# First up projection of a transformer block: one group of modulation columns computed on GpSimd, block products from feature tile 6 instead of 8

## The chip, the core and the metric

The kernel runs on one core of a Trainium2 chip. A core has TensorE (PE in the profile; PEld is its weight load), VectorE (DVE), ScalarE (ACT), GpSimd (POOL) and SyncE (SP, which issues the transfers). They run their own instruction streams, each in order, and wait for each other through semaphores. The metric is device time in microseconds: the median of 3 runs of the kernel before is 1021.51 us (1021.45 to 1022.29).

## The reference, cut to what matters

One layer of a streaming encoder on 512 frames of width 1024: a gated feed-forward net, a token mixer, a second gated feed-forward net. Before each, the input is normalised and scaled and shifted by columns that a linear layer makes from one conditioning vector `c`.

```python
sc = jax.nn.silu(c)
mod = sc @ w_ada[l] + b_ada[l]                # 1024 x (9 * 1024)
sh1, s1, g1, sh2, s2, g2, sh3, s3, g3 = jnp.split(mod, N_MOD, axis=-1)
h = _modulate(x, sh1, s1)                     # rms(x) * (1 + s1) + sh1
x = x + 0.5 * g1 * _swiglu(h, ffn1_w_in[l], ffn1_w_out[l])
# _swiglu: gate, up = split(h @ w_in, 2);  (silu(gate) * up) @ w_out
```

`sh1` and `s1` are needed before anything else. The other seven vectors (14 pieces of 512 columns) are needed later: `g1` when the first feed-forward net's output is added to `x`, the rest after that. A "group" is four pieces, so group 0 is `g1` and `sh2`.

## The kernel before, in words

Everything is kept transposed: features on the 128 partitions, the 512 frames along the row. The hidden width of the feed-forward net, 2816, is 22 feature tiles of 128. For each tile f the gate part and the up part need a product of a 1024 x 128 slice of weights with the 1024 x 512 input `h`. Products are in float32 accuracy made of three reduced products: weights and input are each split into a high and a low part, and high*high, high*low and low*high are added up in PSUM (`mm3`). ScalarE rounds to the high part, VectorE subtracts to get the low part.

The first up projection (`ffn1`) has four stages. `phase0` makes the shift and scale, the input and tiles 0 to 2. `plain` makes tiles directly: per tile 2 parts x 8 slices x 3 = 48 matmuls of 512 columns (L475 to L477). `by_sevens` makes tiles by a Strassen-like scheme: the gate and up weights and the two halves of the frames form a 2 x 2 block product, done with seven products instead of eight, each 4 slices x 3 = 12 matmuls of 256 columns, so 84 per tile (L360). The seven products need sums and differences of the inputs, made once (`combined`: tiles t, th, tl), and of the weights, made for each tile (`sevenths`, one tile ahead, in place in the weight buffers wr, and split into wh, wl, sh, sl). Last, tile 21 is plain again while the activations are split. Before, tiles 3 to 7 are plain and 8 to 20 go by sevens.

The modulation columns of group 0 are made as side work. `ada_rest` loads pieces of `w_ada` (128 x 512, tile ar), multiplies each by its entry of `sc` and accumulates eight of them into a sum aa, all on VectorE: L842 for the first, L844 for the others, 32 instructions for the group. `ada_columns` then lets TensorE add up the partitions of the four sums (L866), ScalarE copy the result and TensorE transpose it (L873), and VectorE add the bias. Before, the sums of group 0 stand between the matmuls of plain tiles 3 to 6 and the columns in tile 7.

What sets the order: side work is a Python generator, and `Rates` decides how many of its steps are placed between two pieces of main work. From the code written in that order a scheduler makes each engine's stream. Most 128 x 512 tiles share 56 slots (`slots`); a tile that gets a used slot waits for the slot's last reader. Weight tiles wr have four buffers, so the pair of tile f+2 is loaded when that of tile f is no longer read. All these transfers stand in one queue, SP's.

Of the kernel before, what the change touches and what calls it, by code (L numbers as in the profile page):

```python
# [11 lines left out]
F32 = mybir.dt.float32  # L12
# [4 lines left out]
ALU = mybir.AluOpType  # L17
AX = mybir.AxisListType

P = 128  # L20
NT = 512
D = 1024
KT = D // P
# [3 lines left out]
EPS = 1e-6  # L27
HALF = NT // 2
KPARTS = ((0, 8), (8, 8), (16, 6))
SEVEN = range(8, 21), range(4, 21)  # L30
PAD = 112
SEVENS = 0, 1
PLAN = (("all", 0), ("all", 1), ("tail", 4), ("tail", 5), ("tail", 6), ("tail", 7), (0, 4), (0, 6), ("most", 2), ("most", 3),
# [66 lines left out]
class Block:  # L100
# [712 lines left out]
        return self.rsqrt(ve, n)  # L813


    def ada_rest(self, groups, late=False):


        nc = self.nc
        a1 = self.ins["w_ada"][0]  # L820
        waiting = None

        def pair(kc, o):
            src = a1[kc * P:(kc + 2) * P, o:o + NT]
            if late:
                a = [self.slot(s="ar") for _ in range(2)]
                for e in range(2):
                    self.load(a[e], src[e * P:(e + 1) * P])
                return a
            a = self.early.tile([P, 2, NT], F32, tag="ar", name=self.name("ar"), bufs=3)  # L830
            self.load(a, src.rearrange("(k p) n -> p k n", p=P))
            return [a[:, e] for e in range(2)]

        for g in groups:
            accs = []
            for c in range(4 * g, min(4 * g + 4, 14)):
                acc = self.slot(s="aa")
                for kc in range(0, KT, 2):
                    for e, a in enumerate(pair(kc, 2 * D + c * NT)):
                        sc = self.sc[:, kc + e:kc + e + 1]  # L840
                        if kc + e == 0:
                            nc.vector.tensor_scalar(out=acc, in0=a, scalar1=sc, scalar2=None, op0=ALU.mult)  # L842
                        else:
                            nc.vector.scalar_tensor_tensor(out=acc, in0=a, scalar=sc, in1=acc, op0=ALU.mult, op1=ALU.add)  # L844
                    yield
                    if waiting and kc in (2, 4):
                        if next(waiting, "end") == "end":
                            waiting = None
                accs.append(acc)
            waiting = self.ada_columns(g, accs)  # L850
        if not late:
            self.columns = waiting
            return
        yield
        yield
        for _ in waiting:
            yield
            yield
# [59 lines left out]
    def ffn1(self):  # L918
        with self.tc.tile_pool(name="p0", bufs=3) as self.p0:
            with self.in_order():  # L920
                pu = self.phase0()
        self.late_pool = self.tc.tile_pool(name="early", bufs=4)
        self.early = self.late_pool.__enter__()
        with self.behind():
            act = [self.glu(pu[f], pu[3 + f], whole=True) for f in range(3)]
        side, sums = Side(), Side()
        side.add(self.ada_rest((0,)))
        sums.add(self.combined())
        with self.behind():
            self.plain(act, 3, 4, Rates((side,), (0.75,)))  # L930
            self.plain(act, 4, 6, Rates((side, sums), (0.75, 1)))
        self.plain(act, 6, 7, Rates((side, sums), (1, 1)))
        side.flush()
        self.late_exit()
        self.seven_enter()
        side.add(self.columns)
        self.plain(act, 7, 8, Rates((sums, side), (1, 0.1)), True)
        sums.flush()
        side.flush()
        self.by_sevens(act, SEVEN[0])  # L940
        return act

    def plain(self, act, f0, f1, side, last=False):
# [14 lines left out]
        self.late_pool = self.tc.tile_pool(name="seven", bufs=2)  # L958
        self.seven = self.late_pool.__enter__()

    def by_sevens(self, act, fs):

        side, self.last_queued = Side(), None

        def first():
            yield
            yield
            self.prefetch(1)

        for f in fs:  # L970
            w = self.weights7
            if f + 1 in fs:
                side.add(self.next_unit(ahead=0))
            else:
                side.add(first())
            if f + 2 == fs.stop:
                self.preload(2)
            with self.queued(mybir.EngineType.Activation, self.last_queued):
                act.append(self.seven_products(w, side))
                side.flush()  # L980
        self.late_exit()
        self.late_enter(12)
        last = fs[-1] + 1
        self.whole = act[:8]

        def parted():
            for i in range(last):
                act[i] = self.glu_parts(act[i], 8 <= i < 14)
                yield

        side.add(parted())
        for f in range(last, FT):
            p = []
            for _ in range(2):
                u, q = self.next_unit(), self.acc()
                for k in (0, 4):
                    self.dense(q, u, self.h, k0=k, k1=k + 4)
                    side.step(3)
                p.append(q)
            act.append(self.glu(*p))  # L1000
        self.splits = side

    def down(self, act, gate, norm=None):
# [27 lines left out]

        last = KT - 1
        side, held = Side(), []
        side.add(self.ada_rest((1, 2) if norm else (3,), True))
        if norm:
            self.consts = Side()
            self.consts.add(self.mixer_consts())
# [98 lines left out]
    def last_down(self, act, gate):  # L1136

        nc = self.nc
        full = slice(0, NT)
        side, sums, parts7, ended, held = Side(), Side(), Side(), [], []  # L1140
        side.add(self.ada_rest((3,), True))
        sums.add(self.act_sums(self.whole))

        def update(t, ts, src):
            nc.vector.scalar_tensor_tensor(out=self.xT[t][:, ts], in0=src, scalar=self.mod[gate][:, t:t + 1],
                                           in1=self.xT[t][:, ts], op0=ALU.mult, op1=ALU.add)

        def ahead():
            self.preload(1)
            parts7.add(self.raws.pop(0)())  # L1150

        def stores():
            while ended:
                self.store(ended.pop(0), range(NB))
                yield

        for at, (kind, t) in enumerate(PLAN):
            after = [k for k, _ in PLAN[at + 1:at + 3]] + ["all"] * 2
            if kind in SEVENS:
                w, work = self.weights7, parts7  # L1160
                if after[0] in SEVENS:
                    ahead()
                else:
                    work = Side()
                    work.add(self.readied())
                self.seven_down(w, act, 8 * kind, t, update, work, stores())
                work.flush()
                if kind:
                    ended += [t, t + 1]
                elif after[0] not in SEVENS:  # L1170
                    sums.add(self.act_sums(act[8:16]))
                continue
            p = self.acc()
            for i, (k0, n) in enumerate(KPARTS):
                if i in MISSING[kind]:
                    continue
                u = self.next_unit(ahead=0 if i == 2 and after[0] in SEVENS else 1)
                if kind == "tail" and after[0] == "tail" and after[1] in SEVENS or (
                        i == (0 if kind == "most" else 1) and after[0] in SEVENS):
                    ahead()  # L1180
                if at == 2:
                    side.flush()
                for k in range(0, n, 2):
                    while not at and any(not isinstance(a, tuple) for a in act[:k0 + k + 5]):
                        self.splits.step()
                    for j in range(k, k + 2):
                        xh, xl = act[k0 + j]
                        self.mm3(p, u[0][:, j, :], u[1][:, j, :], xh, xl, k0 + j == (16 if kind == "tail" else 0),
                                 k0 + j == FT - 1)
                    if at == 1:  # L1190
                        side.step()
                    if at > 1 or i == 2 and at:
                        sums.step()
                    parts7.step()
                if ended and kind != "tail":
                    self.store(ended.pop(0), range(NB))
            held.append((t, p))
            if at > 1:
                for h, p in held:
                    update(h, full, p)  # L1200
                    if kind == "all" or h < 2:
                        ended.append(h)
                held = []
            if after[0] in SEVENS:
                sums.flush()
                parts7.flush()
# [1296 lines left out]
```

## Time and profile before

| | |
|---|---|
| median of 3 runs | 1021.51 us |
| the profiled execution | 1021.74 us, span 1020.0 us |
| TensorE (PE) busy | 1010.3 us, 99% |
| VectorE (DVE) busy | 809.1 us, 79% |
| ScalarE (ACT) busy | 513.5 us, 50% |
| GpSimd (POOL) busy | 28.9 us, 3% |
| plain tiles of the first up projection | about 58 to 114 us |
| tiles by sevens | about 114 to 245 us |

Times in a view are microseconds from the start of the span, mean durations of one instruction are in nanoseconds. Matmuls overlap, so the time of a row of them is read from start to start, not from the duration of one. A row of the windows view gives for a stretch its length and, for each engine, busy time and the number of instructions, then the granted TensorE clock and the share of the transfer engines. A row of the timeline gives start, duration, engine, line, operation, output and inputs with shapes, the count, and in brackets the idle time before it and what ended it.

### The profile page before, as it was taken

The page shows a single profiled execution, that of the slowest core. Times are in us where ns is not written, and L with a number is a line of the kernel's source. Part 1 is how long each engine was busy: PE and PEld are TensorE (multiplying, and loading weights), DVE is VectorE, ACT ScalarE, POOL GpSimd, SP SyncE. Part 2 cuts the span into 40 slices and gives each one's busy share as a digit, 9 for nine tenths or more (in the row PEclk, how much of TensorE's full clock was granted, in tenths as well). Part 3 has the DMA queues.
Part 4 walks back from the last instruction along what each step waited for, and adds up shares of the span by engine and source line. Part 5 has one row for each costly group of instructions (what it writes and reads, how often), then busy time and mean ns, then how long its engine had stood idle before and what let it go on. Part 6 is the DMA issues. An engine that isn't in the chain of part 4 may idle for free.

```text
span 1020.0 us, 17205 instructions
## 1 busy us (share of the span) xinstructions
PE 1010.3 (99%) x6729; PEld 908.1 (89%) x6729; DVE 809.1 (79%) x1428; ACT 513.5 (50%) x921; POOL 28.9 (3%) x74
## 2 busy tenths in 40 slices
PE   7999999999999999999999999999999999999998
PEld 6788899999887899888888888998999999987988
DVE  4789788887787847878988658777888888789995
ACT  4453455556422225558846465464555555634443
POOL 0000000000200000100000011000000000000000
PEclk9999999999999999999999999999999999999999
DMA  9998233333688835321222210213233333372612
GB/s 326 291 280 263 63 104 108 100 115 110 187 295 292 284 74 173 82 62 42 67 73 52 70 36 21 84 49 96 85 102 106 107 102 110 113 253 72 175 42 63
DMA packets 203775, 130.79 MB, mean 128 GB/s; under 512 B 14241, under 2 KB 188334, under 8 KB 203694
## 3 DMA queue, kind: packets, MB, share of 16 engines
q1 hardware_dynamic: 203694, 129.70, 42.1%
q8 instruction: 53, 0.87, 0.3%
q14 instruction: 28, 0.23, 0.1%
HBM read 127.18 MB, written 2.49 MB: 127 GB/s over the span
## 4 chain that ended last, share of the span: by engine, by line
PE 95%; DVE 3%; DMA 1%; issue 0%; ACT 0%; SPq 0%; POOL 0%; DVEq 0%
PE pa L360 17%; PE pa L475 16%; PE pa L476 15%; PE pa L477 15%; PE pb L360 13%; PE pa L1228 3%; PE pb L1228 2%; PE pb L2186 1%; PE pb L2166 1%; PE pb L475 1%; PE pb L476 1%; PE pb L477 1%; PE pb L1735 1%; PE pb L673 1%; DMA vecs<-in_b_ada 1%; DVE cv L1679 1%
## 5 line engine op out<-in xcount | busy, mean ns | idle before, releaser
L275 DVE TENSOR_TENSOR wl<-wr,wh 128x1024 fp32r<-128x1024 f32 x105 | 128.2, 1222 | 45.1 <-ACT wh L279 45.0
L234 ACT CAST wh<-wr 128x1024 fp32r<-128x1024 f32 (+1 forms) x87 | 87.3, 1012 | 146.5 <-PE pa L476 121.3
L475 PE MATMUL pa<-hh,wh 128*128 128x512 f32 (+1 forms) x357 | 137.2, 384 | 0.0
L477 PE MATMUL pa<-hh,wl 128*128 128x512 f32 (+1 forms) x357 | 134.9, 378 | 0.0
L476 PE MATMUL pa<-hl,wh 128*128 128x512 f32 (+1 forms) x357 | 134.7, 377 | 0.0
L235 DVE TENSOR_TENSOR wl<-wr,wh 128x1024 fp32r<-128x1024 f32 (+1 forms) x87 | 101.5, 1172 | 41.3 <-ACT wh L234 41.1
L279 ACT CAST wh<-wr 128x1024 fp32r<-128x1024 f32 x105 | 107.4, 1052 | 13.0 <-DVE wr L275 7.2
L475 PE MATMUL pa<-ah,wh 128*128 128x512 f32 (+1 forms) x294 | 110.5, 376 | 0.0
L476 PE MATMUL pa<-al,wh 128*128 128x512 f32 (+1 forms) x294 | 110.1, 374 | 0.0
L477 PE MATMUL pa<-ah,wl 128*128 128x512 f32 (+1 forms) x294 | 109.7, 373 | 0.0
L475 PEld LDWEIGHTS pa<-hh,wh 128*128 128x128 f32 x357 | 67.3, 189 | 13.1 <-issue 1.6
L844 DVE SCALAR_TENSOR_TENSOR aa<-ar,sc,aa 128x512 f32<-128x512 f32 x98 | 73.5, 750 | 6.8 <-DMA ar<-in_w_ada 4.9
L477 PEld LDWEIGHTS pa<-hh,wl 128*128 128x128 f32 x357 | 67.2, 188 | 12.0
L476 PEld LDWEIGHTS pa<-hl,wh 128*128 128x128 f32 x357 | 67.3, 189 | 10.7
L275 DVE TENSOR_TENSOR wr<-wr,wr 128x512 f32<-128x512 f32 x105 | 72.5, 690 | 2.0
L360 PE MATMUL pa<-hh,wh 128*128 128x256 f32 x240 | 68.0, 283 | 0.0
L360 PE MATMUL pa<-th,wh 128*128 128x256 f32 x240 | 67.9, 283 | 0.0
L360 PE MATMUL pa<-tl,wh 128*128 128x256 f32 x240 | 67.9, 283 | 0.0
L360 PE MATMUL pa<-th,wl 128*128 128x256 f32 x240 | 67.9, 283 | 0.0
L360 PE MATMUL pa<-hl,wh 128*128 128x256 f32 x240 | 67.9, 283 | 0.0
L360 PE MATMUL pa<-hh,wl 128*128 128x256 f32 x240 | 67.9, 283 | 0.0
L475 PEld LDWEIGHTS pa<-ah,wh 128*128 128x128 f32 x294 | 55.3, 188 | 12.2 <-ACT wh L234 2.5
(485 smaller groups left out, 2619.1 us busy)
## 6 DMA issues: line engine op xcount, KB each, us to landing
wr<-in_ffn_w_in SPq DMA_DIRECT2D x79, 512.0 KB
ar<-in_w_ada SPq DMA_DIRECT2D x96, 256.0 KB
wr<-in_ffn_w_out SPq DMA_DIRECT2D x32, 512.0 KB
ar<-in_w_ada SPq DMA_DIRECT2D x22, 512.0 KB
wr<-in_w_in SPq DMA_DIRECT2D x21, 512.0 KB
wr<-in_ffn_w_out SPq DMA_DIRECT2D x16, 384.0 KB
wr<-in_w_out SPq DMA_DIRECT2D x8, 512.0 KB
wr<-in_ffn_w_in SPq DMA_DIRECT2D x8, 384.0 KB
```

What stands on the lines that cost most here:

```text
L234: self.nc.scalar.copy(hi, raw)
L235: self.nc.vector.tensor_tensor(out=lo, in0=raw, in1=hi.bitcast(F32), op=ALU.subtract)
L275: sub = lambda out, x, y: nc.vector.tensor_tensor(out=out, in0=x, in1=y, op=ALU.subtract)
L279: nc.scalar.copy(hi[:, :n], raw[:, :n])
L360: nc.tensor.matmul(z, a[:, j, :], b, start=start and j == 0 and i == 0, stop=j == 3 and i == 2, skip_group_check=not start)
L475: mm(out, wh, xh, start=start, stop=False)
L476: mm(out, wh, xl, start=False, stop=False)
L477: mm(out, wl, xh, start=False, stop=stop)
L673: nc.tensor.matmul(pg[32 * q:32 * q + 32, :256], self.sc[:, kc:kc + 1].to_broadcast([P, 32]), a[kc], start=(e == 0), stop=(e == 1), tile_p ...
L844: nc.vector.scalar_tensor_tensor(out=acc, in0=a, scalar=sc, in1=acc, op0=ALU.mult, op1=ALU.add)
L1228: nc.tensor.matmul(z, a[:, j, :], b, start=start and j == 0 and i == 0, stop=j == 3 and i == 2, skip_group_check=not start)
L1679: nc.vector.scalar_tensor_tensor(out=a[:, d:], in0=p[:, :NT - d], scalar=wj(3 - d), in1=a[:, d:], op0=ALU.mult, op1=ALU.add)
```

## The change

The first range of `SEVEN` is now 6 to 20, so tiles 6 and 7 go by sevens and only tiles 3 to 5 are plain. The side work of those plain tiles is now `combined` alone. The modulation columns of group 0 move into `by_sevens`: `ada_first` takes the sums from `ada_sums(..., pooled=True)`, waits six steps and takes the columns. It is placed at 0.4 steps for each step of the main side work, so about 2.4 steps a tile. With `pooled` the sums are made by GpSimd, in two instructions for each piece (a multiplication in place, L826, and an addition, L828; the first piece of a sum needs only L826). Groups 1 to 3 stay on VectorE with the same instructions. The pieces are now loaded one by one (256 KB) into slots, not in pairs into a pool of their own.

```diff
-SEVEN = range(8, 21), range(4, 21)
+SEVEN = range(6, 21), range(4, 21)
...
+    def ada_sums(self, group, accs, pooled=False):
+        g, v = self.nc.gpsimd, self.nc.vector
+        for c in range(4 * group, min(4 * group + 4, 14)):
+            acc = self.slot(s="aa")
+            for kc in range(KT):
+                a = self.slot(s="ar")
+                self.load(a, self.ins["w_ada"][0][kc * P:(kc + 1) * P, 2 * D + c * NT:2 * D + c * NT + NT])
+                sc = self.sc[:, kc:kc + 1]
+                if pooled:
+                    g.tensor_scalar(out=acc if kc == 0 else a, in0=a, scalar1=sc, scalar2=None, op0=ALU.mult)
+                    if kc:
+                        g.tensor_tensor(out=acc, in0=acc, in1=a, op=ALU.add)
+                elif kc == 0:
+                    v.tensor_scalar(out=acc, in0=a, scalar1=sc, scalar2=None, op0=ALU.mult)
+                else:
+                    v.scalar_tensor_tensor(out=acc, in0=a, scalar=sc, in1=acc, op0=ALU.mult, op1=ALU.add)
+                if kc % 2:
+                    yield
+            accs.append(acc)
+
+    def ada_first(self):
+        accs = []
+        yield from self.ada_sums(0, accs, True)
+        for _ in range(6):
+            yield
+        for _ in self.ada_columns(0, accs):
+            for _ in range(3):
+                yield
...
-        self.late_pool = self.tc.tile_pool(name="early", bufs=4)
-        self.early = self.late_pool.__enter__()
+        self.seven_enter()
         with self.behind():
             act = [self.glu(pu[f], pu[3 + f], whole=True) for f in range(3)]
-        side, sums = Side(), Side()
-        side.add(self.ada_rest((0,)))
+        sums = Side()
         sums.add(self.combined())
         with self.behind():
-            self.plain(act, 3, 4, Rates((side,), (0.75,)))
-            self.plain(act, 4, 6, Rates((side, sums), (0.75, 1)))
-        self.plain(act, 6, 7, Rates((side, sums), (1, 1)))
-        side.flush()
-        self.late_exit()
-        self.seven_enter()
-        side.add(self.columns)
-        self.plain(act, 7, 8, Rates((sums, side), (1, 0.1)), True)
+            self.plain(act, 3, 5, sums)
+        self.plain(act, 5, 6, sums, True)
         sums.flush()
-        side.flush()
-        self.by_sevens(act, SEVEN[0])
+        self.by_sevens(act, SEVEN[0], (self.ada_first(),))
...
+        side, other, self.last_queued = Side(), Side(), None
+        other.add(*others)
+        both = Rates((side, other), (1, 0.4))
...
-                act.append(self.seven_products(w, side))
+                act.append(self.seven_products(w, both))
                 side.flush()
+        other.flush()
```

What this does to the streams, at three places. First GpSimd, behind its first use of the normalisation (`ry`), before:

```order
L220 TENSOR_TENSOR ry_170<-ve_168,mhalf_92 128x4
L1375 MEMSET mk_2981 128x128
L1379 AFFINE_SELECT mk_2981<-ones_90 128x128
```

and now:

```order
L220 TENSOR_TENSOR ry_170<-ve_168,mhalf_92 128x4
L826 TENSOR_SCALAR aa_971<-ar_972,sc_128 128x512
L826 TENSOR_SCALAR ar_975<-ar_975,sc_128 128x512
L828 TENSOR_TENSOR aa_971<-aa_971,ar_975 128x512
L826 TENSOR_SCALAR ar_1014<-ar_1014,sc_128 128x512
L828 TENSOR_TENSOR aa_971<-aa_971,ar_1014 128x512
L826 TENSOR_SCALAR ar_1018<-ar_1018,sc_128 128x512
L828 TENSOR_TENSOR aa_971<-aa_971,ar_1018 128x512
```

GpSimd gets 32 multiplications and 28 additions of 128 x 512 where it had nothing between the start of the kernel and the mixer's masks (mk). On SP's queue their loads stand in eight packets of four, each behind the weight pair of one tile, from the pair of tile 8 to that of tile 15.

Second VectorE, around the start of plain tile 3, before:

```order
L893 TENSOR_TENSOR af_609<-sg_607,pb_257 128x512
L842 TENSOR_SCALAR aa_648<-ar_649,sc_128 128x512
L235 TENSOR_TENSOR wl_699<-wr_696,wh_698 128x1024
L844 SCALAR_TENSOR_TENSOR aa_648<-ar_649,sc_128,aa_648 128x512
L844 SCALAR_TENSOR_TENSOR aa_648<-ar_672,sc_128,aa_648 128x512 x2
L844 SCALAR_TENSOR_TENSOR aa_648<-ar_688,sc_128,aa_648 128x512 x2
L235 TENSOR_TENSOR wl_739<-wr_736,wh_738 128x1024
```

and now:

```order
L235 TENSOR_TENSOR wl_701<-wr_698,wh_700 128x1024
L897 TENSOR_TENSOR af_609<-sg_607,pb_257 128x512
L320 TENSOR_TENSOR t_649<-hm_243 128x256
L320 TENSOR_TENSOR t_650<-hm_434,hm_243 128x256
L320 TENSOR_TENSOR t_649<-hm_434,t_649 128x256
L320 TENSOR_TENSOR t_650<-hm_434,t_649 128x256
L1461 TENSOR_TENSOR tl_687<-t_649,th_686 128x512
```

The 32 accumulations have left VectorE, and the combined inputs (t, tl) begin a tile earlier, directly behind the activations of tiles 0 to 2.

Third TensorE, where the columns are added up, before (inside plain tile 7):

```order
L477 MATMUL pa_1006<-hh_210,wl_933 128x512
L866 MATMUL pb_1047<-aa_648,ones_90 32x512
L866 MATMUL pb_1047<-aa_755,ones_90 32x512
L866 MATMUL pb_1047<-aa_868,ones_90 32x512
L866 MATMUL pb_1047<-aa_967,ones_90 32x512
L475 MATMUL pa_1058<-hh_196,wh_1002 128x512
```

and now (inside tile 17, behind its product 7):

```order
L360 MATMUL pb_2415<-th_839,wl_2392 128x256
L870 MATMUL pb_2485<-aa_971,ones_90 32x512
L870 MATMUL pb_2485<-aa_1255,ones_90 32x512
L870 MATMUL pb_2485<-aa_1539,ones_90 32x512
L870 MATMUL pb_2485<-aa_1823,ones_90 32x512
L360 MATMUL pa_2414<-th_686,wh_2372 128x256
```

The same four instructions stand about ten tiles later; the last of them needs the last GpSimd addition.

More of the change, by code (lines that the diff above doesn't have):

```diff
@@ L813, in rms_cols @@
         return self.rsqrt(ve, n)
-    def ada_rest(self, groups, late=False):
-        nc = self.nc
-        a1 = self.ins["w_ada"][0]
-        waiting = None
[L823 to L832, printed above, removed]
+    def ada_sums(self, group, accs, pooled=False):
[17 more added lines that the diff above has]
+            accs.append(acc)
@@ L834, in ada_rest @@
+    def ada_first(self):
[6 more added lines that the diff above has]
+                yield
+    def ada_rest(self, groups):
+        waiting = None
         for g in groups:
             accs = []
[L836 to L849, printed above, removed]
+            for i, _ in enumerate(self.ada_sums(g, accs)):
+                yield
+                if waiting and i % 4 in (1, 2):
+                    if next(waiting, "end") == "end":
+                        waiting = None
@@ L850, in ada_rest @@
             waiting = self.ada_columns(g, accs)
-        if not late:
-            self.columns = waiting
-            return
         yield
@@ L959, in seven_enter, with by_sevens @@
         self.seven = self.late_pool.__enter__()
-    def by_sevens(self, act, fs):
-        side, self.last_queued = Side(), None
+    def by_sevens(self, act, fs, others=()):
+        side, other, self.last_queued = Side(), Side(), None
+        other.add(*others)
+        both = Rates((side, other), (1, 0.4))
         def first():
@@ L1033, in down @@
         side, held = Side(), []
-        side.add(self.ada_rest((1, 2) if norm else (3,), True))
+        side.add(self.ada_rest((1, 2) if norm else (3,)))
         if norm:
@@ L1140, in last_down @@
         side, sums, parts7, ended, held = Side(), Side(), Side(), [], []
-        side.add(self.ada_rest((3,), True))
+        side.add(self.ada_rest((3,)))
         sums.add(self.act_sums(self.whole))
```

## The prediction, as it was put on record

> **What bounds the kernel now.** I read the page's busy times first, then its chain of waits, then the windows view of the stage that changes.
>
> ```profile
> span 1020.0 us, 17205 instructions
> PE 1010.3 (99%) x6729; PEld 908.1 (89%) x6729; DVE 809.1 (79%) x1428; ACT 513.5 (50%) x921; POOL 28.9 (3%) x74
> PE 95%; DVE 3%; DMA 1%; issue 0%; ACT 0%; SPq 0%; POOL 0%; DVEq 0%
> ```
>
> TensorE is busy for 99% and is 95% of the chain: only TensorE work taken out, or a wait put into it, moves the time. The stretches below are the plain tiles 3, 4 and 5, then the tiles by sevens 9 and 10 from one VectorE weight split to the next.
>
> ```profile
> 58.22:69.10 10.88, 10.88 (x49) 9.01 (x48) 8.87 (x12) 3.59 (x6) 0.00 (x0) 1.00 0.97 307
> 69.10:80.00 10.90, 10.90 (x50) 9.03 (x49) 10.56 (x17) 3.82 (x6) 0.00 (x0) 1.00 0.78 230
> 80.00:90.90 10.90, 10.90 (x50) 9.03 (x49) 10.66 (x18) 3.86 (x6) 0.00 (x0) 1.00 0.91 291
> 127.35:137.43 10.08, 10.08 (x86) 10.08 (x85) 8.47 (x13) 5.56 (x11) 0.00 (x0) 1.00 0.37 106
> 137.43:147.51 10.08, 10.08 (x86) 10.08 (x85) 8.47 (x13) 5.55 (x11) 0.00 (x0) 1.00 0.36 103
> ```
>
> Columns: length, then PE, PEld, DVE, ACT and POOL busy, clock, transfer share, GB/s. A plain tile takes 10.89 us (32.68 over three), a tile by sevens 10.08. In neither does TensorE wait, at full clock. The reader should also see VectorE's 8.47 us of 10.08 in a tile by sevens, with nothing on GpSimd: that is where the change puts 60 GpSimd instructions.
>
> **The change part by part.** I sum against the profiled execution, 1021.74 us (span 1020.0 and 1.74 around it); the median of the runs, 1021.51, is 0.23 lower, which I ignore.
>
> *Two tiles by sevens.* 2 x (10.89 - 10.08) = 1.6 us less TensorE time. This is certain if nothing waits.
>
> *The columns* are the same TensorE, ScalarE and VectorE instructions in another place: 0.
>
> *32 accumulations leave VectorE* in tiles 3 to 7. VectorE was nearly full there (10.66 of 10.90), but TensorE did not wait for it, so this buys 0. It is the cover for the earlier start: the first block weights and the combined inputs must now be ready at 90.9 us, not 114.2.
>
> *The loads.* Eight packets of 4 x 256 KB, one a tile: 1.05 MB in 10.08 us, as much again as the 106 GB/s moved now, so a transfer share near 0.74 instead of 0.37. Behind each packet stands only the next weight pair, which waits for its buffers until the end of the tile anyway: 0, hidden by most of a tile. Without that cover a packet would add 3.7 us, what as many bytes take now (0.37 x 10.08).
>
> *GpSimd beside VectorE* decides the sum. GpSimd's own time is not on the path, but the trace shows that the two engines stop each other. The small power instruction L220 normally lasts 1.01 us. Twice it lasted longer:
>
> ```profile
> 487.34 1.01 POOL L220 TENSOR_TENSOR ry<-ve,mhalf 128x4 f32<-128x4 f32 x1 [43.36 <-DVE ve L812]
> 411.32 0.62 DVE L1550 SCALAR_TENSOR_TENSOR ul<-ur,cwT,uh 128x384 fp32r<-128x384 f32 x1
> 411.48 1.32 POOL L220 TENSOR_TENSOR ry<-ve,mhalf 128x4 f32<-128x4 f32 x1 [22.09 <-DVE ve L812]
> 422.62 0.75 DVE L1550 SCALAR_TENSOR_TENSOR ul<-ur,cwT,uh 128x512 fp32r<-128x512 f32 x1
> 422.76 1.48 POOL L220 TENSOR_TENSOR ry<-ve,mhalf 128x4 f32<-128x4 f32 x1 [9.95 <-DVE ve L812]
> ```
>
> Both times VectorE had just begun an instruction with two inputs in SBUF, and GpSimd's extra 0.31 and 0.47 us end about where that instruction ends. The other way round there is one case, the longest of 44 equal subtractions:
>
> ```profile
> L900 DVE TENSOR_TENSOR al<-af,ah x44: 677/687/803, 247.5 to 904.1; 128x512 fp32r<-128x512 f32 x44
> 260.44 0.33 POOL L1391 TENSOR_SCALAR_AFFINE_SELECT mk<-mk 128x128 f32<-128x128 f32 x1
> 260.47 0.80 DVE L900 TENSOR_TENSOR al<-af,ah 128x512 fp32r<-128x512 f32 x1 [0.69 <-ACT ah L899]
> ```
>
> It began 0.03 us after a GpSimd instruction that reads 128 columns, and lasted 0.12 us more than the median. So I take it that a VectorE instruction with two SBUF inputs and a GpSimd read exclude each other, and that GpSimd gets its turn when the VectorE instruction before it ends.
>
> [...]
>
> How long does one GpSimd instruction keep VectorE out? From below: 0.12 us for 128 columns is 0.46 for 512, so 0.46 for L826 and, with two inputs, 0.93 for L828; the floor under that is 0, if the one case was chance. Less than nothing is excluded, since VectorE has nothing to gain from GpSimd's reads. From above: the whole of the only two-input GpSimd instruction of this size, 1.04 us.
>
> ```profile
> 611.12 1.04 POOL L1467 TENSOR_TENSOR Sg<-S,gl 128x512 f32<-128x512 f32 x1
> L363 DVE TENSOR_TENSOR sg<-pb,z 128x256 f32<-128x256 f32 x13 | 5.4, 419 | 1.2 <-PE pb L360 1.2
> L363 DVE TENSOR_TENSOR up<-pb,z 128x256 f32<-128x256 f32 x13 | 5.4, 418 | 0.0
> 123.03 1.23 DVE L275 TENSOR_TENSOR wl<-wr,wh 128x1024 fp32r<-128x1024 f32 x1 [0.48 <-ACT wh L279]
> 127.23 0.28 PE L360 MATMUL pa<-th,wh 128*128 128x256 f32 x1
> ```
>
> I take 0.46 for L826 (one input, as in the measured case) and 0.98 for L828 (between 0.93 and 1.04): 32 x 0.46 + 28 x 0.98 = 42.1 us. Over the eight tiles that get a packet, VectorE must do 8 x 8.47 = 67.8 us. Of that, two instructions a tile read PSUM and can run beside GpSimd: 8 x 0.84 = 6.7. Together 67.8 + 42.1 - 6.7 = 103.2 us, in 8 x 10.08 = 80.6 us of TensorE work: 22.6 too much. VectorE has a lead: the split that begins at 123.03 ends at 124.26 and is first used at 127.23, so 3.0 us go unseen. Remaining 19.6; less the 1.6 saved, +18.0: 1039.7, say **1040 us**. By the lower row (0.46 and 0.93; 40.7) it is +16.6, 1038; by the upper (1.04 each; 62.4) +38.3, 1060; by the floor -1.6, 1020.
>
> Behind the delayed VectorE splits stand TensorE's products 6, 7 and 3 of the next tile. GpSimd keeps pace: about 7.5 instructions a packet, with 42.1 / 8 = 5.3 us of reading in a tile of some 12.7. Where VectorE waits for a slot that GpSimd read last, one to three tiles lie between, and tile 17's column sums come three tiles behind the last packet: 0.
>
> **The rivals.**
>
> *A, exclusion as summed:* 1040, with 1034 to 1053 as its own range (holds from a little under the lower row to 0.6 and 1.04).
>
> *B, no harm: GpSimd's reads fit into VectorE's gaps.* Each tile has 10.08 - 8.47 = 1.6 us free and 0.84 of PSUM reads, and the lead of 3.0 is there once. So nothing is lost while a packet keeps VectorE out for less than (80.6 + 3.0 - 67.8 + 6.7) / 8 = 2.8 us, 0.37 an instruction. For it: only one row shows VectorE delayed, and by 0.12. Against it: 0.37 is less than that row scales to even for the shorter instruction. Time: 1021.74 - 1.6 = 1020.1, not slower.
>
> *C, each engine keeps the other out for its whole instruction.* With 1.04 for all 60, 1060. Against it: L1391 lasted 0.33 and cost VectorE only 0.12. [...] The trace agrees for VectorE's hold (0.31 and 0.47 to its end), not for GpSimd's.
>
> *D, tile 6 starts late,* because its weights and the combined inputs are not ready at 90.9.
>
> ```profile
> 114.12 0.69 DVE L893 TENSOR_TENSOR af<-sg,pa 128x512 f32<-128x512 f32 x1 [3.41 <-PE pa L477]
> ```
>
> Before, VectorE had finished all that 3.4 us ahead, with 32 accumulations more in the same stretch. Those are gone, but two tiles of time as well. If one tile's whole preparation were late it would cost up to 8.5 - 1.6, about +7 without contention: 1029.
>
> **How the numbers follow.** A 0.66, B 0.20, C 0.08, D 0.06. A measurement tells 0.2%, about 2 us, from no change. B with its -1.6 lies within it, mostly: same 0.20; a little more gain than counted, with a lighter first stage, gives faster 0.04; A, C and D are slower: 0.76. The time is A's, 1040. The range goes from B's 1020 (less half a microsecond) to 1055, most of the way between A's and C's values, since the holds are known only between 0.46 and 1.04.
>
> **What would show it.** In tiles 7 to 15 the windows view should show TensorE busy for less than the stretch, tiles of 11 to 14 us instead of 10.08, back at 10.08 from about tile 16. VectorE's 128x1024 splits, 1.22 us now, should show a mean or a maximum well above it, or idle time in front of them; the PSUM readers should keep 0.42. GpSimd's L826 and L828 should last longer than 1.04 for the additions, waiting for VectorE. Tiles 3 to 5 should stay at 10.89 with no wait ahead of tile 6. I am wrong if L275 keeps 1.22 us and the tiles keep 10.08 beside a busy GpSimd (B), or if TensorE's first wait stands at 90.9 us (D), or if GpSimd finishes so late that TensorE waits at L870.

## The result and the profile after

The changed kernel takes **1040.54 us** (median, 1039.87 to 1040.94) where the kernel before, run beside it, takes 1021.9: a ratio of 1.0185, 95% interval 1.0173 to 1.0197. It is 18.6 us slower; the prediction said 18.0. Its profiled execution has a span of 1039.2 us. The size was right, but the experiments show that two terms behind it were wrong in opposite directions.

The page of the changed kernel: span, busy times, and shares of the chain that ended last.

```profile
span 1039.2 us, 17444 instructions
PE 1015.4 (98%) x6801; PEld 912.7 (88%) x6801; DVE 829.8 (80%) x1414; ACT 518.9 (50%) x935; POOL 141.2 (14%) x134
PE 81%; POOL 8%; DVE 6%; DMA 2%; SPq 1%; issue 1%; ACT 0%; POOLq 0%; DVEq 0%
```

TensorE's share of the chain fell from 95% to 81%, and GpSimd, which had none, has 8%. VectorE lost 32 accumulations, has 14 instructions less in all, and is still 20.7 us busier. The windows of the stage say where (columns as in the prediction: length, then PE, PEld, DVE, ACT and POOL busy, clock, transfer share, GB/s):

```profile
58.22:90.90 32.68, 32.68 (x146) 27.07 (x145) 24.97 (x41) 14.88 (x22) 0.00 (x0) 1.00 0.38 110
121.00:131.00 10.00, 8.78 (x72) 8.37 (x71) 9.93 (x11) 5.25 (x9) 9.83 (x6) 1.00 0.44 137
191.00:201.00 10.00, 6.95 (x46) 6.74 (x45) 8.17 (x9) 2.06 (x4) 9.75 (x7) 0.83 0.33 97
231.00:241.00 10.00, 10.00 (x85) 10.00 (x85) 8.28 (x12) 5.47 (x11) 0.00 (x0) 1.00 0.37 107
```

Plain tiles 3 to 5 run as forecast. From about 125 us TensorE has holes beside a full VectorE and a full GpSimd; one stretch (191 to 201) is worse than the rest, has a lower clock, and VectorE itself stands still in it for 1.8 us. After GpSimd's last instruction the stage is as before. VectorE's groups in this stage (90 to 250 us; last number before the bar: mean ns of one; behind it: idle time ahead and what ended it):

```profile
L275 DVE TENSOR_TENSOR wl<-wr,wh 128x1024 fp32r<-128x1024 f32 x40 | 55.5, 1388 | 5.8 <-ACT wh L279 5.4
L275 DVE TENSOR_TENSOR wr<-wr,wr 128x512 f32<-128x512 f32 x40 | 32.1, 802 | 0.9
L298 DVE TENSOR_TENSOR wr<-wr 128x512 f32<-128x512 f32 x14 | 17.1, 1220 | 0.5
L1465 DVE TENSOR_TENSOR af<-sg,up 128x512 f32<-128x512 f32 x13 | 13.3, 1025 | 2.8 <-POOL aa L828 2.8
L363 DVE TENSOR_TENSOR up<-z 128x256 f32<-128x256 f32 x13 | 12.0, 924 | 0.6 <-ACT z L377 0.6
L275 DVE TENSOR_TENSOR sl<-wr,sh 128x512 fp32r<-128x512 f32 x14 | 12.0, 854 | 0.0
L363 DVE TENSOR_TENSOR sg<-pb,z 128x256 f32<-128x256 f32 x14 | 5.8, 415 | 2.4 <-POOL aa L828 2.4
```

Six kinds have both inputs in SBUF, and all six are longer than undisturbed (1223, 691, 693, 686, 421 and 683 ns, in this order, in the first experiment). The seventh reads PSUM and keeps 0.42 us. Count times extra length, added over the kinds that are longer, is 31.8 us of VectorE time lost. I call this sum the **hold** and use it for every kernel below. The idle column has something else: 5.2 us in which VectorE waited for a buffer that GpSimd had not finished with. GpSimd's groups, in the same stretch:

```profile
L826 POOL TENSOR_SCALAR ar<-ar,sc 128x512 f32<-128x512 f32 x28 | 65.7, 2348 | 5.0 <-DMA ar<-in_w_ada 5.0
L828 POOL TENSOR_TENSOR aa<-aa,ar 128x512 f32<-128x512 f32 x28 | 37.8, 1349 | 2.3
L826 POOL TENSOR_SCALAR aa<-ar,sc 128x512 f32<-128x512 f32 x4 | 9.4, 2360 | 82.1 <-DMA ar<-in_w_ada 82.1
```

Together 112.9 us, or 14.1 for each of the eight packets, where a tile has 10.08. Two pairs from the timeline (start, duration) show how the two engines meet:

```profile
100.85 1.46 POOL L828 TENSOR_TENSOR aa<-aa,ar 128x512 f32<-128x512 f32 x1
101.07 1.52 DVE L363 TENSOR_TENSOR up<-z 128x256 f32<-128x256 f32 x1
105.16 1.29 POOL L828 TENSOR_TENSOR aa<-aa,ar 128x512 f32<-128x512 f32 x1
105.20 1.80 DVE L1465 TENSOR_TENSOR af<-sg,up 128x512 f32<-128x512 f32 x1
```

A 0.42 us VectorE instruction that starts inside a GpSimd addition lasts 1.52, a 0.69 us one lasts 1.80: about 1.1 us more each, and they end 0.3 and 0.6 us behind the addition. Last, the waits in this stage (us in total, times, longest):

```profile
PE pa L360 <- ACT z L365: 7.5, 7, 1.5
PE pa L360 <- ACT z L377: 3.2, 2, 3.1
PE pb L360 <- DVE wl L275: 1.4, 3, 0.5
PE pa L360 <- DVE wl L275: 0.8, 5, 0.2
ACT wh L279 <- DVE wr L275: 31.9, 13, 3.5
```

Only 2.2 of TensorE's 12.9 us are waits for VectorE's splits directly. The larger part, 7.5 us, goes through ScalarE. In order, it waits for VectorE's late weight differences (wr) before it can round them; behind that wait stands its copy of product 1 to SBUF (z, L365), and TensorE's product 6, which adds into the same place in PSUM, needs that copy to be done. The longest wait has another origin, here in order of time:

```profile
191.55 0.69 DVE L1465 TENSOR_TENSOR af<-sg,up 128x512 f32<-128x512 f32 x1 [2.84 <-POOL aa L828]
194.97 0.42 DVE L363 TENSOR_TENSOR sg<-pb,z 128x256 f32<-128x256 f32 x1 [1.18 <-POOL aa L828]
195.43 0.42 ACT L374 ACTIVATE sg<-sg 128x256 f32<-128x256 f32 x1 [4.79 <-DVE sg L363]
196.16 0.38 PE L360 MATMUL pa<-hh,wh 128*128 128x256 f32 x1 [3.05 <-ACT z L377]
```

VectorE twice waits until GpSimd has finished with a buffer, ScalarE waits for what VectorE writes then, and TensorE for the copy that stands behind that on ScalarE. From first matmul to first matmul, tiles 6 to 8 take 10.1 us each, tile 14, with this wait, takes 16.3, and tiles 9 to 16 together take 19.5 us more than eight times 10.08.

### The profile page after: what moved, and what is told of

The parts are those of the page before. It is cut to its first block, busy times and chain, and to the rows that moved or that the text cites. A ratio compares the mean times of both kernels' runs of the same rounds, so it can differ in the third digit from the quotient of the medians.

```text
span 1039.2 us, 17444 instructions
## 1 busy us (share of the span) xinstructions
PE 1015.4 (98%) x6801; PEld 912.7 (88%) x6801; DVE 829.8 (80%) x1414; ACT 518.9 (50%) x935; POOL 141.2 (14%) x134
## 4 chain that ended last, share of the span: by engine, by line
PE 81%; POOL 8%; DVE 6%; DMA 2%; SPq 1%; issue 1%; ACT 0%; POOLq 0%; DVEq 0%
PE pa L475 14%; PE pa L477 14%; PE pa L476 14%; PE pa L360 12%; PE pb L360 9%; POOL ar L826 5%; PE pa L1226 3%; POOL aa L828 2%; PE pb L1226 2%; SPq L139 1%; DMA ar<-in_w_ada 1%; PE pb L2184 1%; PE pb L2164 1%; DMA wr<-in_ffn_w_in 1%; POOL aa L826 1%
## 5 line engine op out<-in xcount | busy, mean ns | idle before, releaser
L275 DVE TENSOR_TENSOR wl<-wr,wh 128x1024 fp32r<-128x1024 f32 x111 | 142.1, 1281 | 34.3 <-ACT wh L279 33.9
L279 ACT CAST wh<-wr 128x1024 fp32r<-128x1024 f32 x111 | 113.8, 1051 | 49.1 <-DVE wr L275 39.1
L475 PE MATMUL pa<-hh,wh 128*128 128x512 f32 (+1 forms) x325 | 124.6, 384 | 0.0
L477 PE MATMUL pa<-hh,wl 128*128 128x512 f32 (+1 forms) x325 | 122.4, 377 | 0.0
L476 PE MATMUL pa<-hl,wh 128*128 128x512 f32 (+1 forms) x325 | 122.2, 376 | 0.0
L275 DVE TENSOR_TENSOR wr<-wr,wr 128x512 f32<-128x512 f32 x111 | 81.0, 730 | 2.2
L475 PEld LDWEIGHTS pa<-hh,wh 128*128 128x128 f32 x325 | 61.3, 189 | 11.1 <-issue 1.6
L477 PEld LDWEIGHTS pa<-hh,wl 128*128 128x128 f32 x325 | 61.2, 188 | 10.7
L476 PEld LDWEIGHTS pa<-hl,wh 128*128 128x128 f32 x325 | 61.3, 189 | 9.5
L826 POOL TENSOR_SCALAR ar<-ar,sc 128x512 f32<-128x512 f32 x28 | 65.7, 2348 | 5.0 <-DMA ar<-in_w_ada 5.0
```

The costliest lines, as they stand in the source:

```text
L275: sub = lambda out, x, y: nc.vector.tensor_tensor(out=out, in0=x, in1=y, op=ALU.subtract)
L279: nc.scalar.copy(hi[:, :n], raw[:, :n])
L475: mm(out, wh, xh, start=start, stop=False)
L476: mm(out, wh, xl, start=False, stop=False)
L477: mm(out, wl, xh, start=False, stop=stop)
L826: g.tensor_scalar(out=acc if kc == 0 else a, in0=a, scalar1=sc, scalar2=None, op0=ALU.mult)
```

## The experiments

Each is an edit of the changed kernel. "Free" is what VectorE has left in the prediction's terms: 80.6 + 3.0 - 67.8 = 15.8 us for sums made within eight tiles (15.9 in the expectations, which round differently).

**Writes only.** All 60 GpSimd instructions become fills of zeros; the sums are left out of the computation, loads, buffers and waits stay.

```diff
-g.tensor_scalar(out=acc if kc == 0 else a, in0=a, scalar1=sc, scalar2=None, op0=ALU.mult)
+g.memset(acc if kc == 0 else a, 0.0)
-g.tensor_tensor(out=acc, in0=acc, in1=a, op=ALU.add)
+g.memset(acc, 0.0)
```

> The changed kernel with every GpSimd instruction of the sums replaced by a memset of the same tile: 60 instructions, all loads, slots and waits stay, but GpSimd only writes and reads nothing. Left out: the sums of group 0 (their columns are wrong). Theory (GpSimd's SBUF reads and VectorE's two-input instructions exclude each other): no exclusion is left, tiles of 10.08 us from tile 6 on, VectorE's 128x1024 split at 1.22 us, 1020.3 us, 1.6 below the kernel before. Rival (the loads, the slots or the earlier start cost it): near 1040 as the changed kernel.

Measured: 1020.38 us, ratio 0.9986 (0.9977 to 0.9995), no TensorE wait in the stage.

```profile
L275 DVE TENSOR_TENSOR wl<-wr,wh 128x1024 fp32r<-128x1024 f32 x42 | 51.4, 1223 | 22.4 <-ACT wh L279 22.4
L826 POOL MEMSET ar<- 128x512 f32 x28 | 14.6, 529 | 76.9 <-DMA ar<-in_w_ada 75.2 <-DVE wl L275 0.8 <-DVE up L363 0.2
```

VectorE keeps its 1.22 us and has 22.4 us of slack ahead of this line again. So the earlier start, the moved columns, the loads and the buffers together give -1.5 us, against the forecast -1.6; all the loss comes with what GpSimd's instructions read or with their length ("pace only", below, keeps the length and takes the reads away). Beside these 60 instructions that only write, 0.53 us each, VectorE's two largest kinds last what they last in the kernel before (wl 1223 and wr 691 ns in both).

**Additions only** and **multiplications only.** The first drops the 28 multiplications in place (the four that begin a sum become fills), the second the 28 additions; both leave that part out of the computation.

```diff
 additions only:        -g.tensor_scalar(out=acc if kc == 0 else a, in0=a, ...)
                        +if kc == 0: g.memset(acc, 0.0)
 multiplications only:  -g.tensor_tensor(out=acc, in0=acc, in1=a, op=ALU.add)
```

> The changed kernel without its 32 GpSimd multiplications (a memset begins each sum; the pieces are added up unscaled): 28 additions of about 1.3 us remain, 5 us a tile, so GpSimd cannot fall behind. Left out: the scaling by the conditioning vector. Theory: an addition keeps VectorE out for about 1.05 us (seen on the delayed instructions of the changed kernel's trace), 28 x 1.05 = 29.4, less the 12.9 + 3.0 us that VectorE has free and in lead, less 1.6: +12, 1034 (1029 to 1036). Rival (the loss is GpSimd's pace, 13.4 us for a packet in tiles of 10.08): 1020.

> The changed kernel without its 28 GpSimd additions: 32 multiplications in place remain, 1.57 us each where nothing stops them. Left out: the adding up of the pieces. Theory: a multiplication keeps VectorE out for 0.1 to 0.46 us, 3 to 15 us in all, inside the 12.9 + 3.0 us that VectorE has free: 1020 to 1021. Rival (an engine keeps the other out for its whole instruction): 32 x 1.57 = 50, so +33, 1053.

Measured: 1032.83 us (ratio 1.0108, 1.0093 to 1.0123) and 1019.98 us (0.9982, 0.9973 to 0.9992). Two rows of each, additions first:

```profile
L275 DVE TENSOR_TENSOR wl<-wr,wh 128x1024 fp32r<-128x1024 f32 x42 | 62.1, 1479 | 8.1 <-ACT wh L279 7.4
L829 POOL TENSOR_TENSOR aa<-aa,ar 128x512 f32<-128x512 f32 x28 | 49.3, 1761 | 76.6 <-DMA ar<-in_w_ada 74.9
```

```profile
L275 DVE TENSOR_TENSOR wl<-wr,wh 128x1024 fp32r<-128x1024 f32 x42 | 53.0, 1263 | 18.7 <-ACT wh L279 18.7
L826 POOL TENSOR_SCALAR ar<-ar,sc 128x512 f32<-128x512 f32 x28 | 53.3, 1919 | 16.3 <-DMA ar<-in_w_ada 13.5 <-DVE up L363 2.8
```

The hold of the additions is 26.0 us, 0.93 each (forecast 0.98). That of the multiplications is 3.7 us, 0.12 each (forecast 0.46, or the whole instruction by rival C). A multiplication is not short, its shortest lasts 1.57 us; here it is the one that gives way, with 1.92 us on average. One by one the rows say the same: in the first kernel 28 VectorE instructions with two SBUF inputs begin inside an addition, and each is 0.67 to 1.10 us late; in the second some 50 begin inside a multiplication, half of them are not late at all, and none by more than 0.38. Against the kernel before the two kernels are +10.9 and -1.9 us, the change +18.6. These times need not add up, since each kernel has the free 15.8 us to itself; the holds should, and 26.0 + 3.7 = 29.7 is 2.1 short of 31.8, and the 5.2 us of waits for GpSimd's buffers occur in neither.

**Half additions.** As additions only, on the left 256 columns; the multiplications and the right halves are left out.

```diff
-g.tensor_tensor(out=acc, in0=acc, in1=a, op=ALU.add)
+g.tensor_tensor(out=acc[:, :HALF], in0=acc[:, :HALF], in1=a[:, :HALF], op=ALU.add)
```

> As the kernel with the additions alone, but each adds the left 256 columns only (the multiplications and the right halves are left out of the computation). If an addition holds VectorE in proportion to its length: 28 x 0.47 = 13 us, below the 15.9 us free, so about 1020.5 (to 1022). If it holds it for the same time whatever its length (a fixed price of one start): 1032.8 as with whole additions. If only the longer VectorE instruction beside it counts: between, 1024 to 1028.

Measured: 1020.15 us, ratio 0.9984 (0.9974 to 0.9994).

```profile
L275 DVE TENSOR_TENSOR wl<-wr,wh 128x1024 fp32r<-128x1024 f32 x42 | 57.3, 1365 | 12.2 <-ACT wh L279 11.6
```

The hold is 10.3 us, 0.37 an addition instead of 0.93. It falls with the length, to 0.4 of the whole addition's for half the columns, and below the free 15.8 us it costs nothing.

**On VectorE.** The sums at the same places, with VectorE's fused instruction.

```diff
-yield from self.ada_sums(0, accs, True)
+yield from self.ada_sums(0, accs)
```

> The changed kernel with the sums of group 0 made on VectorE at the same places (one instruction for each piece, 32 in all; the same result). Theory: each takes VectorE's time alone, 0.66 us from start to start, 21 us in all, of which 15.9 are free or lead: +5 - 1.6, about 1025. If VectorE's gaps behind ScalarE cannot be filled, 21 - 1.6: 1041, no better than on GpSimd.

Measured: 1024.95 us, ratio 1.0032 (1.0019 to 1.0044). Doing the sums itself takes 22.9 us of VectorE's time (21.0 + 1.9), where GpSimd's help costs it 31.8; the kernel is 3.0 us slower than before instead of 18.6.

**Pace only.** Fills again, four for each multiplication and three for each addition, so that GpSimd is as long at work as in the changed kernel but reads nothing; the sums are left out.

```diff
-g.tensor_scalar(out=acc if kc == 0 else a, in0=a, ...)
+for _ in range(4): g.memset(acc if kc == 0 else a, 0.0)
-g.tensor_tensor(out=acc, in0=acc, in1=a, op=ALU.add)
+for _ in range(3): g.memset(acc, 0.0)
```

> Every GpSimd multiplication becomes 4 fills of zeros into the same buffer and every addition 3, so that GpSimd is as busy as in the changed kernel (32 x 4 x 0.528 + 28 x 3 x 0.528 = 112 us against its 113 us) and falls behind in the same way, but reads no SBUF; loads, buffers and waits stay, the sums themselves are left out (the columns come from zeros). Theory (held VectorE instructions make 12 to 13 us, GpSimd falling behind the rest): 1021 to 1027, VectorE durations as before (wl 1.22 us), some waits for GpSimd. Rival (GpSimd's pace is what sets the tiles' time, as the chain through its instructions could be read): 1035 to 1041.

Measured: 1020.14 us, ratio 0.9985 (0.9976 to 0.9994), no TensorE wait and no VectorE wait for GpSimd, which was at work to about 196 us. That is below the expected 1021, and the expected waits did not come: by this, falling behind costs nothing.

**Paced additions** and **paced multiplications.** The same with only one kind replaced: additions beside four fills, multiplications beside three fills. The other kind is left out of the computation.

> The changed kernel with each GpSimd multiplication replaced by 4 fills of the same buffer (4 x 0.53 = 2.1 us, near the 2.35 us of the multiplications beside VectorE), the additions kept; the products by the condition vector are left out. GpSimd is as far behind as in the changed kernel, but only the additions hold VectorE (26 us as with additions alone). Theory A (falling behind makes VectorE wait for GpSimd's buffers, 5.2 us in the changed kernel, and that is what it has over the additions alone): 1036 to 1039, with waits of VectorE for GpSimd. Theory B (falling behind costs nothing here either; the multiplications make the rest): 1032 to 1034. Additions that follow each other without a gap could also hold VectorE longer than those that wait for loads: then wl and the others are above their 1.48 and 0.81 us.

> The changed kernel with each GpSimd addition replaced by 3 fills of the same buffer (3 x 0.53 = 1.6 us, near the addition's 1.35), the multiplications kept; the additions are left out of the computation. GpSimd is then as busy and as far behind as in the changed kernel, but nothing reads two inputs. Theory (the multiplications alone delay VectorE by 0.12 us each, whatever the pace; the 10 us that the changed kernel has over the paced additions, 1030.57, come only where additions and multiplications meet): 32 x 0.12 = 3.8 us against 15.9 free, so 1020 to 1021, wl at 1.26 us or less. Rival (multiplications that follow each other without loads to wait for cost VectorE what the prediction took, 0.46 each, and GpSimd's lateness adds): 14.7 us, near all of the 15.9 free, and 2 to 6 us of waits: 1023 to 1028.

Measured: 1030.57 us (ratio 1.0087, 1.0073 to 1.0101) and 1024.62 us (1.0031, 1.0019 to 1.0044). From the additions, VectorE's group and its wait; then from the multiplications VectorE's group and the waits of VectorE and TensorE:

```profile
L275 DVE TENSOR_TENSOR wl<-wr,wh 128x1024 fp32r<-128x1024 f32 x42 | 55.7, 1327 | 6.7 <-ACT wh L279 5.9
DVE af L1466 <- POOL aa L829: 1.8, 1, 1.8
```

```profile
L275 DVE TENSOR_TENSOR wl<-wr,wh 128x1024 fp32r<-128x1024 f32 x42 | 53.9, 1283 | 12.1 <-ACT wh L279 11.2
DVE af L1466 <- POOL ar L826: 6.0, 2, 3.7
DVE sg L363 <- POOL ar L826: 1.5, 1, 1.5
PE pa L360 <- ACT z L377: 3.0, 1, 3.0
```

The holds are 25.6 us (0.91 an addition) and 6.6 us (0.21 a multiplication): 32.2 together, near the 31.8 of the changed kernel. The additions' 1030.57 lies below both theories; of the waits that theory A expected, 1.8 us came. The multiplications' 6.6 us lie inside the free 15.8 and should cost nothing, so their +3.6, 5.2 above "writes only", come from elsewhere: VectorE stood 7.5 us for buffers that a late GpSimd still held, and TensorE waited 3.3 us in all, 3.0 of it behind that. The remaining 1.9 us stay open; in the profiled execution tile 6 already begins 1.2 us later than in "pace only", ahead of any such wait. Theory and rival both fell here, the theory on the time, the rival on the hold. Nor does "pace only" settle the matter: counted from the start of tile 6, GpSimd ended its fifth to seventh packets there 1 to 3 us earlier, and no buffer was missed. I take it that falling behind is free up to a point and then costs whole waits; where that point lies was not tested.

**Spread on GpSimd.** All as changed, but over 13 tiles instead of eight.

```diff
-both = Rates((side, other), (1, 0.4))
+both = Rates((side, other), (1, 0.26))
-        for _ in range(6):            # idle steps before the columns
-            yield
+        yield
         for _ in self.ada_columns(0, accs):
-            for _ in range(3):
-                yield
+            yield
```

> The changed kernel with its GpSimd sums at 0.26 instead of 0.4 of a step, so over 13 tiles instead of 8, and the idle steps between the sums and the columns cut from 6 to 1 and from 3 to 1. Theory with the holds as the runs so far have them (0.94 us for an addition, 0.12 us for a multiplication): 28 x 0.94 + 32 x 0.12 = 30.2 us against 13 x 1.61 + 3.0 = 23.9 us free, 6.3 us over, less the 1.5 us of the earlier start: about 1026.7 (1023 to 1029), multiplications and additions 2.6 x 2.35 + 2.3 x 1.35 = 9.2 us in a tile of 10.08, so that GpSimd keeps pace. Rival (the sizes of the prediction, 0.46 and 0.98 us): 13 x 8.47 + 42.1 - 6.7 - 13 x 10.08 - 3.0 = 11.5, so 1031.9.

Measured: 1031.77 us, ratio 1.0101 (1.0086 to 1.0116).

```profile
L275 DVE TENSOR_TENSOR wl<-wr,wh 128x1024 fp32r<-128x1024 f32 x42 | 62.4, 1486 | 3.2 <-ACT wh L279 2.8
L828 POOL TENSOR_TENSOR aa<-aa,ar 128x512 f32<-128x512 f32 x28 | 41.0, 1464 | 2.3
```

No VectorE instruction waits for GpSimd now, and TensorE's longest wait is 1.0 us. The hold is 34.8 us, not the 30.2 that the single-kind kernels had led me to; 34.8 - 23.9 free - 1.6 = 9.3, measured 9.9. The expected 1026.7 was missed by the hold; why it is larger here than in the changed kernel stays open. The prediction's sizes hit this time because their sum, 35.4 net, was near 34.8, not because 0.46 was right for a multiplication.

**Spread on VectorE**, and **the same with loads ahead.** The first is the spread with VectorE's instructions, two at each step; the second issues each load four instructions before its use, and also places the instructions one at a time (2.5 a tile).

```diff
+        more = loads()                # slot, load, ahead.append(a), yield
+        for _ in range(4): next(more)
...
+                next(more, None)
+                a = ahead.pop(0)
...
+                yield                 # after each instruction
...
-        both = Rates((side, other), (1, 0.4))
+        both = Rates((side, other), (1, 0.5))
```

> The same spread over 13 tiles with the sums on VectorE: 28 fused instructions of 0.75 us and 4 of 0.48, 22.9 us against 23.9 us free. Theory (only the free time of VectorE counts): no delay, and the earlier start stays: 1020.4 (1019.6 to 1021.5). Rival (an instruction put into a tile makes what follows it late wherever free time lies): about 1023, between this and the 1024.95 of the sums on VectorE over 8 tiles.

> The sums spread on VectorE as in the kernel that spread them over 13 tiles (1025.59), one instruction at a time (2.5 in a tile), and each load issued four instructions before its use instead of right before it. Theory (there 7.8 us of waits of VectorE for the loads of the ar tiles made the time, 22.9 + 7.8 against 23.9 us free): the waits go, 22.9 against 23.9 us, and what is left is the earlier start: about 1020.4 (1019.6 to 1021.5). Rival (VectorE's own instructions are late however they are spread, the waits ended inside free time): 1024 to 1026.

Measured: 1025.59 us (ratio 1.0040, 1.0025 to 1.0055) and **1020.22 us** (0.9985, 0.9976 to 0.9994). The accumulations in the one and the other:

```profile
L832 DVE SCALAR_TENSOR_TENSOR aa<-ar,sc,aa 128x512 f32<-128x512 f32 x28 | 20.9, 748 | 7.8 <-DMA ar<-in_w_ada 7.8
```

```profile
L863 DVE SCALAR_TENSOR_TENSOR aa<-ar,sc,aa 128x512 f32<-128x512 f32 x28 | 21.0, 750 | 0.1
```

Spreading alone missed its expected 1020.4, since the loads came just too late for an in-order VectorE: 22.9 + 7.8 us against 23.9 free. With the loads ahead the waits for them go, and TensorE never waits in this stage. What placing the instructions one at a time gave beside that was not tried by itself. This version leaves nothing of the computation out and is below both kernels, though by 0.15% against the kernel before, less than the 0.2% that the prediction takes as telling a change. It keeps all that the earlier start can give.

## Why the prediction was right

| | hold | VectorE waits for GpSimd | free | sum with -1.6 | measured against before |
|---|---|---|---|---|---|
| changed kernel | 31.8 | 5.2 | 15.8 | +19.6 | +18.6 |
| additions only | 26.0 | 0 | 15.8 | +8.6 | +10.9 |
| paced additions | 25.6 | 1.8 | 15.8 | +10.0 | +8.8 |
| spread on GpSimd | 34.8 | 0 | 23.9 | +9.3 | +9.9 |

Where the hold exceeds the free time, the prediction's way of summing, with the waits added, holds to within 2.3 us. The sum leaves out what TensorE lost at half clock (last section), about 1.5 us in the changed kernel; how much of that reaches the end is not shown. By the prediction's steps:

- *Two tiles by sevens, columns, loads, accumulations leaving VectorE* (-1.6, 0, 0, 0): right, -1.5 in one run. Rival D is out: TensorE reaches tile 6 without a wait.
- *Exclusion of VectorE's two-input instructions and GpSimd's reads*: right in kind, and rival B is out. 42.1 us less 6.7 for PSUM readers is 35.4 net; measured 31.8. The terms in it were mis-sized. The step "0.46 for L826", scaled from one case of 0.12 us beside 128 columns, failed: a multiplication cost 0.12 alone and 0.21 at pace. An addition, 0.98 less its share of the PSUM relief, measured 0.91 to 0.93 after all relief, so it was somewhat too low. The 1.04 us taken as its upper length was too short as well: the shortest here is 1.26.
- *Rival C, the whole instruction*: for additions not far off. VectorE instructions with two SBUF inputs that start in one are 0.7 to 1.1 us late, beside 1.3 to 1.5 that it lasts. For multiplications it is wrong, 0.21 of at least 1.57.
- *"GpSimd keeps pace ... 0"*: this step failed. It took the 5.3 us that a packet should keep VectorE out as the time that GpSimd needs for it. A packet took 14.1 us, because the multiplication, thought the cheap one, lasts 1.57 us undisturbed and 2.35 beside VectorE. VectorE stood 5.2 us for GpSimd's buffers. TensorE's longest wait, 3.05 us, comes from them; the paced multiplications, with a hold that fits into the free time, show such a wait again, and the spread kernel, without them, follows the sum of holds alone.

So the forecast 35.4 was really 31.8 of holds and 5.2 of waits, 37.0. The mechanism was right; that the time came within 0.6 us is in part luck, a term too large beside a term left out. How much of the 5.2 us the changed kernel would save with buffers of its own for GpSimd stays open; that was not tried.

Of the signs named ahead, the longer L275, the unmoved PSUM readers and tiles 3 to 5 came as told. Slow tiles came too, but in tiles 9 to 16, not from 7 on, and one of them took 16.3 us, above the 14 named. One sign did not come: additions longer than 1.04 were to show GpSimd waiting, but their 1.35 is nearly their undisturbed length; the waiting shows in the multiplications. And the column sums (L870) did not wait, since six idle steps lie ahead of them. One figure ahead of the prediction is wrong: a tile has five places for side work, so 0.4 gives 2.0 steps a tile, not 2.4; the prediction's eight packets are right.

## What to carry to other kernels

Work handed to an idle GpSimd was paid for here by VectorE's instructions with both inputs in SBUF while GpSimd read there: 60 GpSimd instructions took 31.8 us from a VectorE that could have done the same sums in 22.9. Price the two-input instructions by their length (here 0.91 to 0.93 us for an addition of 512 columns, 0.37 for one of 256), look whether GpSimd's own packet fits into a tile (14.1 us against 10.08), and compare with spreading the work thinly on VectorE, with loads issued early enough that the in-order engine never meets an unfinished one (7.8 us of waits in front of the accumulations without that, 0.1 with it).

## What was not expected of the hardware

On GpSimd the one-input multiplication by a column (1.57 us at least, 128 x 512) is slower than the two-input addition (1.26 at least), and only the addition keeps VectorE out for most of its length (0.91 to 0.93 us, the multiplication for 0.12 to 0.21).

A wait of TensorE cost more than itself here. Behind its longest wait in the changed kernel the granted clock is 0.50 for 3.4 us. A matmul of 256 columns starts every 0.214 us there (197.00 to 200.21 us) and every 0.120 at 1.00, so by these numbers about 1.5 us are lost. With additions only it is 0.50 for 6.8 us, with the paced additions for 3.4. The length of a wait alone does not decide: one of 2.18 us (paced additions) did this, while waits of 2.75 (additions only) and 2.99 us (paced multiplications) left the clock at 1.00. Its place in time accounts for every case here. In each of the three traces the clock, once it has risen (at 9.18, 9.13 and 8.78 us), falls and recovers after a whole number of stretches of 3.413 us: 55 and 56 in the changed kernel, 41 and 43 with additions only, 54 and 55 with the paced additions. The windows on this grid, first of the changed kernel, then with additions only:

```profile
193.50:196.91 3.41, 0.76 (x6) 0.76 (x7) 2.19 (x5) 0.68 (x2) 3.24 (x4) 1.00 0.17 52
196.91:200.32 3.41, 3.41 (x18) 3.41 (x18) 3.34 (x4) 0.71 (x1) 3.33 (x3) 0.50 0.02 5
```

```profile
121.77:125.18 3.41, 1.60 (x14) 1.39 (x12) 3.38 (x4) 1.76 (x2) 1.98 (x2) 1.00 0.00 0
145.67:149.08 3.41, 0.86 (x8) 0.66 (x6) 3.38 (x4) 2.04 (x3) 1.70 (x2) 1.00 0.00 0
149.08:152.49 3.41, 2.76 (x13) 2.76 (x14) 3.41 (x5) 2.06 (x5) 0.00 (x0) 0.50 0.49 144
152.49:155.91 3.42, 3.42 (x18) 3.42 (x18) 3.32 (x7) 1.02 (x3) 0.00 (x0) 0.50 0.95 288
```

Then one of the paced additions, and one of the paced multiplications:

```profile
189.69:193.10 3.41, 1.23 (x11) 1.03 (x10) 3.27 (x6) 2.64 (x5) 3.35 (x8) 1.00 0.00 0
179.42:182.83 3.41, 1.67 (x14) 1.47 (x13) 1.82 (x2) 0.00 (x0) 3.35 (x5) 1.00 0.67 200
```

A stretch in which TensorE stood for 2.65, 2.55 or 2.18 us (3.41 less its busy time) was followed by one at 0.50; after 1.81 and 1.74 us the clock stayed at 1.00, since the grid cuts the waits of 2.75 and 2.99 us in two. It came back after one stretch at half clock without a wait, and after two where the first still held 0.65 us of waiting. Where between 1.81 and 2.18 us the line lies, no run here tells. The clock fell after stretches in which TensorE still worked for 0.76 to 1.23 us.
